# A hybrid attention block on one core: first loads in halves, a different rank for the written-out order, last scalings moved to ScalarE

## The chip, the cores and the metric

The kernel runs on one core of a Trainium2 chip. The core has five engines that run side by side and meet at semaphores: TensorE (PE; its weight loads are listed as PEld), VectorE (DVE), ScalarE (ACT), GpSimd (POOL) and SyncE (SP), which here only issues DMAs. ACT and POOL can issue DMAs as well, each on a queue of its own. The metric is the device time of one execution in microseconds (us), lower is better. Three runs of the kernel before took 426.47, 428.28 and 426.45 us; their median is 426.47.

## What is computed

One layer of an encoder on x of 512 tokens by 1024 channels, all in float32:

```python
h = rmsnorm(x, norm_g)
(q_lat, c_kv, k_rope, z_a, q_b, k_b, v_b, z_b,
 q_idx, k_idx, w_idx, gate_a, gate_b) = split(h @ w_in)
# branch a: 8 heads of latent attention, chunk-causal (chunks of 64)
q  = rmsnorm(q_lat) @ w_uq ; kv = rmsnorm(c_kv) @ w_ukv ; rotary part added
y_a = softmax(mask(q k)) v * silu(z_a)
# branch b: an indexer scores keys, each query keeps its 128 best ones
score = sum_h relu(q_idx_h k_idx) * w_idx_h ; keep the top 128
y_b = softmax(kept(q_b k_b) + rel_bias) v_b * silu(z_b)
merged = sigmoid(gate_a) * (y_a @ w_o_a) + sigmoid(gate_b) * (y_b @ w_o_b)
out = rmsnorm(x + merged @ w_out, final_g)
```

## The kernel before

**Precision.** A float32 product is made of three products of rounded operands. Each operand is split into a high part (rounded by a copy on ACT, `act`) and a low part (the rest, a subtraction on DVE or POOL, `lo_part`, or `stt` where a scale goes with it, as in `split_scaled`). `mm3` (line 405) issues high*high, high*low and low*high into one PSUM bank. So nearly every matmul waits for an ACT instruction and for a DVE instruction behind it.

**Who sets the order.** The order of each engine's instructions is written out while the kernel is built, by a planner (`Flow`, lines 134 to 242). The work is a set of generator functions, each spawned as a thread with a priority, which yield steps (`Step`: one or more engines that could do it, with a duration each), requests for buffers (`Get`) and conditions (`Until`). `Flow.run` (line 183) repeatedly takes the step with the smallest key: the planned start, which `Flow.start` works out from when the engine is free and when operands were written and read, plus a small term for the priority and a random nudge drawn from the seed `DRAW` (71). It emits that instruction and books its planned end. The engines then run their lists in order on the chip, whatever the true durations are. DMAs on SP have a planned queue too (`hw`, `dma`).

**The head.** `loads` (line 528) issues on SP, for each of the eight 128-row slices of transposed x, the slice (`xT`, 256 KB) and the weights of the first projections: `w_qi` for the indexer's queries (256 columns) and `w_kvl` for latents, indexer keys and weights (328 columns). The very first `w_qi` goes on ACT's queue (`setup`, line 484). `setup_pool` (line 502) issues `ident` (for transposes) and `g_lat` on POOL's queue; the planner places them after the fourth slice, but in POOL's own list only two memsets stand ahead of them. `warm_up` gives PE 15 products of zeros. `early_x` (line 618) scales each slice by norm_g and splits it; the first slice's high part is made in three column pieces (256 to 512, 128 to 256, 0 to 128: `PIECES`) and its low part as a whole. `early_w` (line 633) splits the weights through `split_w` (line 605). `early_mm` (line 646) runs the products slice by slice: for the first, high*high of the indexer's queries by pieces, then with the low parts, then the 328 columns for four token tiles with `mm3`; for each later slice six and twelve products.

**The middle.** `fetcher`, `splitter` and `multiplier` walk a list of weight jobs (`QUEUE`). Attention heads run in two lanes per branch beside them: scores, softmax, transposes on PE (`turn`, line 412), a split of the transposed probabilities (`s_ph`), products with the values. Selecting the best keys is a chain of DVE instructions (`topk`, lines 818 to 830). The eight tiles of branch a's gate, after their tanh on ACT (`gate`, line 1170), are stored to DRAM by SP (line 1184) and fetched back later.

**The tail.** `output` (line 1814) computes the last product by a scheme of seven block products. For each token tile, `finish` (line 1760) adds the product to x, has the square summed (`square` on ACT, or, for the last piece, a DVE reduction at line 1768), and multiplies by the final gain. `scale_out` (line 1786) adds the sums, takes the power -0.5 on POOL (`power`, line 374), scales the first half of the columns on DVE and the second on ACT, and stores each half from SP. The tiles end in the order 2, 3, 0, 1; tiles 1 and 3 have three pieces each, tiles 0 and 2 two.

Of the kernel before, what the change touches and what calls it, by code (L numbers as in the profile page):

```python
# [133 lines left out]
class Flow:  # L134
# [9 lines left out]
    def __init__(self):  # L144
        self.free = {"PE": 0.6, "ACT": 0.6, "DVE": 0.6, "POOL": 0.6, "SP": 0.6}
        self.hw, self.dma = 0.6, 0.0
        self.pbias = -1.0
        self.port = 0.0
        self.threads = []

        self.draw = random.Random(DRAW)

# [30 lines left out]
    def run(self, stop=None):  # L183
        while self.threads:
# [15 lines left out]
            for t in self.threads:  # L200
                if isinstance(t.req, Step):
                    for i, (eng, dur, emit) in enumerate(t.req.options):
                        s = self.start(t.req, eng)
                        key = (s + BIAS * t.prio + t.nudge, t.prio)
# [22 lines left out]
            else:  # L227
# [3 lines left out]
                if step.moves and eng == "ACT":  # L231

                    end += 1.8 + step.moves
# [14 lines left out]
DRAW = 71  # L248
# [4 lines left out]
def tile_block(ctx: ExitStack, tc: tile.TileContext, a: dict, out: bass.AP, bias_dram: bass.AP):  # L253
# [181 lines left out]
    def act_dma(dst, src):  # L435
        step = Step([("ACT", 0.06, lambda: nc.scalar.dma_start(dst.ap, src))], bufs(dst), [])
        step.moves = 4.0 * dst.n * dst.ap.shape[0] / 360000
        return step
# [89 lines left out]
    def loads():  # L528
        for kp in range(4):
            for kk in range(2):  # L530
                k = 2 * kp + kk
                x = yield slot("x")
                yield dma(x.all.f, a["xT"][k])
                xt[k] = x
                if k == 0:
                    yield dma(normg.all, a["norm_g"])
                if kp == 0:
                    cq, ck = slice(256 * kk, 256 * kk + 256), slice(328 * kk, 328 * kk + 328)
                    if k:
                        rq = yield slot("er")  # L540
                        yield dma(rq.all.f[:, :256], a["w_qi"][kp][:, cq])
                        eraw["q", k] = rq.all.f[:, :256], True
# [11 lines left out]
            if kp == XAT:  # L554
                spawn(x_squares(), PSQ)
                yield is_done("x loads")
# [48 lines left out]
    def split_w(raw, w, dst, key, cls="w", cap=None, release=False, early=False):  # L605
# [3 lines left out]
        yield act(hi[:, :w], raw)  # L609
# [6 lines left out]
    first_x = {}  # L616

    def early_x():
        for k in range(NK):
            yield Until(lambda: k in xt)  # L620
            hi = yield slot("xg")
            lo = yield slot("xg")
            if k == 0:

                for piece in PIECES:
                    yield act(hi[:, piece], xt[k].all.f[:, piece], AF.Copy, scale=normg[:, k : k + 1])
                    first_x[piece.start] = hi
                yield stt(lo.all, xt[k].all.f, normg[:, k : k + 1], hi.all.f, ALU.mult, ALU.subtract)
# [4 lines left out]
    def early_w():  # L633
        for k in range(NK):
# [3 lines left out]
            yield Until(lambda: ("kv", k) in eraw)  # L638
            raw, last = eraw["kv", k]
            yield from split_w(raw, 328, ewkv, k, "w", WCAP, last, True)  # L640
# [5 lines left out]
    def early_mm():  # L646
# [6 lines left out]
        for i, piece in enumerate(PIECES[:2]):  # L653
            yield Until(lambda: piece.start in first_x)
            for m in range(2):
                yield mm(qi_ps[m][:, piece], [(ewq[0][0][:, m * P : m * P + P], first_x[piece.start][:, piece])], not i, False)
        for k in range(NK):
            yield Until(lambda: k in xg and k in ewq)

            xk = cut(xg[k], SCORED)  # L660
            w = [cut(ewq[k], slice(m * P, m * P + P)) for m in range(2)]
            if k == 0:

                for cw, cx in ((1, 0), (0, 1)):
                    for m in range(2):
                        yield mm(qi_ps[m][:, SCORED], [(w[m][cw], xk[cx])], False, False)
            else:
                for m in range(2):
                    yield mm3(qi_ps[m][:, SCORED], w[m], xk, False, k == NK - 1)
# [4 lines left out]
            for t in range(NT):  # L674
                yield mm3(kv_ps[t][:, :328], cut(xg[k], TOK[t]), cut(ewkv[k], slice(0, 328)), k == 0, k == NK - 1)
# [494 lines left out]
    def gate(name, c, how=proj):  # L1170


        def take(ps):
# [7 lines left out]
            if c in away and name == "w_ga":  # L1181
                yield dma(spilt(c), s.all.f)
# [525 lines left out]
    def out_job(product, c):  # L1708
# [3 lines left out]
        def prep(job):  # L1712
# [47 lines left out]
    def finish(t, half, c0, c1, ps, nth, last, keep=False):  # L1760
# [6 lines left out]
        if last:  # L1767
            step = Step([("DVE", 0.1 + 0.00104 * r.n, lambda: nc.vector.tensor_tensor_reduce(
                junk.tile[:, : r.n], r.ap, r.ap, op0=ALU.mult, op1=ALU.add, scale=1.0, scalar=0.0,
                accum_out=ssf[t].tile[:, nth : nth + 1]))], [junk, ssf[t]], bufs(r))  # L1770
# [4 lines left out]
        else:  # L1775
            spawn(square(t, r, nth), 0)
# [3 lines left out]
        done.add(("g", t, nth))  # L1780

# [4 lines left out]
    def scale_out(t, count):  # L1786
# [3 lines left out]
        yield ts(rs[:, 0:1], ssf[t][:, 0:1], ssf[t][:, 1:2], D * EPS, ALU.add, ALU.add)  # L1790
        if count == 3:
            yield is_done(("sq", t, 2))
            yield tt(rs[:, 0:1], rs[:, 0:1], ssf[t][:, 2:3], ALU.add)
        done.add(("sum", t))
        yield power(rs[:, 0:1])
        yield Until(lambda: all(("g", t, i) in done for i in range(count)))
        for half, engs in ((0, ("DVE",)), (1, ("ACT",))):
            x = rg[t, half].all.f
            yield scale_by(x, x, rs[:, 0:1], engs)
            yield dma(out[TOK[t], half * 512 : (half + 1) * 512], x)  # L1800
# [157 lines left out]
NWARM = 15  # L1958
# [101 lines left out]
```

## Time and profile before

| what | value |
|---|---|
| median of three runs | 426.47 us |
| the profiled execution, whole | 427.16 us |
| its span, first to last instruction | 425.4 us |
| mean granted TensorE clock | 0.995 |
| PE, PEld, DVE, ACT, POOL busy | 98%, 86%, 89%, 62%, 26% |
| HBM read and written | 50.49 MB, 4.21 MB |

The profile is of one execution. An engine's busy time is the time in which at least one of its instructions ran. The ends of matmuls are modelled, and they overlap, so a busy PE isn't PE at its full rate; the distance between starts says more. In a timeline each row has a start, a length, engine, line, operation, what is written and read, and in brackets the engine's idle time before it with what ended it. A line is often that of a helper (L400 is every matmul, L302 and L311 every ACT copy or activation, L328 and L339 the DVE operations, L427 every DMA from SP), so the names of the tiles tell more: `s_xg` is the scaled x of the head, `s_w` a split weight, `s_x` a raw slice, `s_er` and `raw` raw weights, `s_p` probabilities, `sm` small columns, `s_rg` the finished rows.

### The profile page before, as it was taken

What the parts mean: (1) busy time and instruction counts of PE and PEld (TensorE: products, weight loads), DVE (VectorE), ACT (ScalarE), POOL (GpSimd) and SP (SyncE); (2) the same over time, 40 slices, a digit from 0 to 9 for tenths busy, and PEclk for the clock granted to TensorE, in tenths of its full rate; (3) what the DMA queues carried; (4) which work ended last, traced back from release to release, by engine and by line L of the source; (5) the groups of instructions that cost most, each with busy time, mean ns of one, the idle gap of its engine ahead of it and who ended that gap; (6) DMA issues with size and microseconds to landing.
All of it is one profiled execution on the core that took longest, in us unless ns stands there. A gap on an engine that the chain in (4) does not pass through costs nothing.

```text
span 425.4 us, 7106 instructions
## 1 busy us (share of the span) xinstructions
PE 415.3 (98%) x2313; PEld 363.9 (86%) x2313; DVE 380.5 (89%) x815; ACT 262.2 (62%) x587; POOL 109.5 (26%) x131
## 2 busy tenths in 40 slices
PE   8999999999999999999999999999999999999993
PEld 6999868889888888888899988998998888888883
DVE  4789899999999999999879888988799757999995
ACT  6778786585573758544864677494598524436624
POOL 1037865455355723121300101000010002210212
PEclk9999999999999999999999999999999999999998
DMA  8973137817255450285243525425523887453705
GB/s 258 394 278 112 52 100 207 230 45 186 82 139 148 127 160 1 79 256 173 63 128 121 171 79 157 146 65 178 146 79 124 266 322 252 143 180 106 242 0 197
DMA packets 30277, 65.89 MB, mean 155 GB/s; under 512 B 4648, under 2 KB 5688, under 8 KB 30240
## 3 DMA queue, kind: packets, MB, share of 16 engines
q1 hardware_dynamic: 29264, 64.08, 48.5%
q0 software_dynamic: 832, 1.22, 0.9%
q8 instruction: 18, 0.29, 0.3%
q14 instruction: 19, 0.16, 0.1%
q10 hardware_dynamic: 144, 0.13, 0.1%
HBM read 50.49 MB, written 4.21 MB: 129 GB/s over the span
## 4 chain that ended last, share of the span: by engine, by line
PE 54%; DVE 30%; DMA 7%; ACT 4%; issue 4%; POOL 0%; POOLq 0%; SPq 0%; DVEq 0%; ACTq 0%
PE ps L400 50%; DVE mask L826 4%; DMA raw<-w_out 4%; DVE sm L825 3%; PE ps L417 2%; DVE sm L1474 2%; DVE s_ph L328 2%; DVE s_mg L328 2%; DVE s_wsum L328 1%; DMA s_sig<-bias_scratch 1%; DVE s_tmp L328 1%; ACT s_p L311 1%; DVE s_pair L328 1%; DVE s_wo L328 1%; DVE s_w L328 1%
## 5 line engine op out<-in xcount | busy, mean ns | idle before, releaser
L400 PE MATMUL ps<-s_h,s_w 128*128 128x512 f32 (+1 forms) x732 | 170.9, 379 | 0.0
L400 PEld LDWEIGHTS ps<-s_h,s_w 128*128 128x128 f32 x732 | 127.8, 189 | 21.8 <-issue 0.3
L302 ACT CAST s_w<-raw 128x512 fp32r<-128x512 f32 (+3 forms) x124 | 71.6, 593 | 17.8 <-DVE raw L328 9.2
L330 POOL TENSOR_TENSOR s_w<-raw,s_w 128x512 fp32r<-128x512 f32 (+2 forms) x35 | 44.7, 1284 | 130.1 <-ACT s_w L302 123.9
L328 DVE TENSOR_TENSOR s_w<-raw,s_w 128x512 fp32r<-128x512 f32 (+2 forms) x89 | 58.7, 670 | 5.3 <-ACT s_w L302 4.7
L400 PE MATMUL ps<-s_ys,s_w 128*128 128x512 f32 x192 | 43.7, 389 | 0.0
L400 PEld LDWEIGHTS ps<-s_ys,s_w 128*128 128x128 f32 x192 | 36.0, 188 | 7.5
L311 ACT ACTIVATE s_p<-s_p,sm 128x384 f32<-128x384 f32 (+3 forms) x54 | 29.2, 559 | 6.8 <-DVE sm L1571 5.6
L400 PE MATMUL ps<-s_wo,s_mg 128*128 128x512 f32 (+1 forms) x156 | 33.0, 373 | 0.0
L400 PE MATMUL ps<-s_w,s_xg 128*128 128x328 f32 (+1 forms) x192 | 32.5, 323 | 0.0
L400 PEld LDWEIGHTS ps<-s_wo,s_mg 128*128 128x128 f32 x156 | 27.6, 188 | 5.2
L400 PEld LDWEIGHTS ps<-s_w,s_xg 128*128 128x128 f32 x192 | 31.4, 188 | 0.0
L328 DVE TENSOR_TENSOR s_ph<-ps,s_ph 128x384 fp32r<-128x384 f32 (+1 forms) x48 | 27.4, 590 | 2.5 <-ACT s_ph L302 2.3
L302 ACT CAST s_ph<-ps 128x384 fp32r<-128x384 f32 (+1 forms) x48 | 23.5, 514 | 5.5 <-PE ps L417 4.2
L311 ACT ACTIVATE s_p<-ps,sm 128x128 f32<-128x128 f32 (+3 forms) x32 | 16.8, 527 | 15.5 <-DVE sm L1474 15.1
L826 DVE MATCH_REPLACE8 mask<-sm,mask 128x384 f32<-128x384 f32 (+2 forms) x48 | 25.8, 540 | 0.0
L825 DVE MAX8 sm<-mask 128x8 f32<-128x384 f32 (+2 forms) x48 | 25.5, 547 | 0.1
L400 PE MATMUL ps<-s_ph,vv 128*128 128x512 f32 (+3 forms) x128 | 24.9, 325 | 0.0
L417 PE MATMUL ps<-ident,s_p 128*128 128x128 f32 x160 | 24.2, 275 | 0.5 <-DVE s_p L358 0.3
L417 PEld LDWEIGHTS ps<-ident,s_p 128*128 128x128 f32 x160 | 18.8, 140 | 4.7 <-ACT s_p L311 1.0
L400 PEld LDWEIGHTS ps<-s_ph,vv 128*128 128x128 f32 x128 | 20.6, 189 | 2.1 <-DVE s_ph L328 0.2
L400 PE MATMUL ps<-s_lat,s_w 128*128 128x512 f32 x78 | 20.5, 398 | 0.0
(197 smaller groups left out, 737.5 us busy)
## 6 DMA issues: line engine op xcount, KB each, us to landing
raw<-w_out SPq DMA_DIRECT2D x18, 512.0 KB, 4.0
s_op<-s_op SPq DMA_DIRECT2D x36, 128.0 KB, 2.3
raw<-w_ga SPq DMA_DIRECT2D x8, 512.0 KB, 4.5
raw<-w_gb SPq DMA_DIRECT2D x8, 512.0 KB, 4.4
raw<-w_o SPq DMA_DIRECT2D x16, 256.0 KB
s_x<-xT SPq DMA_DIRECT2D x8, 256.0 KB, 4.9
s_xn<-x SPq DMA_DIRECT2D x8, 256.0 KB, 5.7
bias_scratch<-s_sig SPq DMA_DIRECT2D x8, 256.0 KB, 2.5
```

Of the source, the lines that this page charges most:

```text
L302: nc.scalar.copy(dst.ap, src.ap)
L311: nc.scalar.activation(dst.ap, src.ap, func, **kw)
L328: opts.append(("DVE", 0.07 + 0.00104 * x.n, lambda: nc.vector.tensor_tensor(dst.ap, x.ap, y.ap, op=op)))
L330: opts.append(("POOL", 0.15 + 0.0021 * x.n, lambda: nc.gpsimd.tensor_tensor(dst.ap, x.ap, y.ap, op=op)))
L400: nc.tensor.matmul(ps.ap, l.ap, r.ap, start=start and i == 0, stop=stop and i == len(pairs) - 1, skip_group_check=more)
L417: nc.tensor.transpose(d.ap, s.ap, ident.tile)
L825: yield Step([("DVE", t, lambda: nc.vector.max(m8.tile, work.tile))], [m8], [work])
L826: yield Step([("DVE", t, lambda: nc.vector.match_replace(work.tile, m8.tile, work.tile, MARK))], [work], [m8])
L1474: yield Step([("DVE", 0.07 + 0.00104 * n, lambda: nc.vector.tensor_reduce(mx.tile[:, 1:2], ps.tile[:, :n], op=ALU.max, axis=AX.X, negate=T ...
```

## The change

- **First x.** Slice 0 is loaded as two column halves into one tile: columns 256 to 512 by SP, columns 0 to 256 by ACT, behind `w_qi`. `early_x` makes high and low part piece by piece. `early_mm` takes the products of slice 0 piece by piece, with high*high and low*high of the 328 columns ahead of high*low, tile 3 first. The cast of the first `w_kvl` waits in the plan for the pieces of x.
- **First w_qi.** Its high part is made on DVE with a multiplication by 1, not on ACT.
- **ident and g_lat** are issued by SP, behind all slices of x.
- **Order.** The key of a PE or SP step uses `settled`: the time at which its operands will have been left alone by other engines for 2 us (PE; 1 us after SP) or 1 us (SP). The planned start itself isn't changed. `DRAW` is 53, `NWARM` 14, and the planner books ACT's DMAs as a queue.
- **Gate stores** of branch a are issued by ACT.
- **Tail.** The squares on ACT get priority -50. For tile 1 the DVE reduction of its last piece starts from the sum of the other pieces, so the addition behind it goes. Tile 0's first half is scaled on ACT. Tile 1's second half is stored from ACT.
- In the weights of the last product, product 4's sums wait in the plan until product 6's are split.

```diff
+    def settled(self, step, eng, start):
+        s = start
+        for b in (*step.ins, *step.outs):
+            for e, t in ((b.by, b.w), *b.reads.items()):
+                if e != eng and e in SETTLE[eng]:
+                    s = max(s, t + self.lat(e, eng) + SETTLE[eng][e])
+        return s
...
-                        key = (s + BIAS * t.prio + t.nudge, t.prio)
+                        key = ((self.settled(t.req, eng, s) if eng in SETTLE and s < math.inf else s) + BIAS * t.prio + t.nudge, t.prio)
...
-DRAW = 71
+DRAW = 53
+PSQUARE = -50
+SETTLE = {'PE': {'DVE': 2.0, 'ACT': 2.0, 'POOL': 2.0, 'SP': 1.0}, 'SP': {'DVE': 1.0, 'ACT': 1.0, 'POOL': 1.0}}
...
+    def act_move(dst, src):
+        d = dst.ap if isinstance(dst, View) else dst
+        step = Step([("ACT", 0.3, lambda: nc.scalar.dma_start(d, src.ap))], bufs(dst), bufs(src))
...
         eraw["q", 0] = rq.all.f[:, :256], True
+        yield Until(lambda: x0)
+        x0.append(Buf(x0[0].tile, "x0"))
+        yield act_dma(x0[1].all.f[:, LO], a["xT"][0][:, LO])
+        xt[0] = x0[0]
...
-        yield Until(lambda: 3 in xt)
-        yield from pool_dma(ident.all, a["ident"])
-        yield from pool_dma(glat.all, a["g_lat"])
...
+                    yield dma(x.all.f[:, HI], a["xT"][0][:, HI])
+                    x0.append(x)
...
             if kp == XAT:
+                yield dma(ident.all, a["ident"])
+                yield dma(glat.all, a["g_lat"])
...
+        if dst is ewq and key == 0:
+            yield Step([("DVE", 0.1 + 0.00052 * w, lambda: nc.vector.tensor_scalar(
+                hi.tile[:, :w], raw.ap, 1.0, None, ALU.mult))], [hi], bufs(raw))
+        else:
+            yield act(hi[:, :w], raw)
...
+                    yield act(part[0][:, piece], x, AF.Copy, scale=normg[:, 0:1])
+                    first_x[i] = part
+                    yield stt(part[1][:, piece], x, normg[:, 0:1], part[0][:, piece].f, ALU.mult, ALU.subtract)
...
-            yield Until(lambda: ("kv", k) in eraw)
+            yield Until(lambda: ("kv", k) in eraw and len(first_x) == len(PIECES))
...
+                for t in (3, 2, 1, 0):
+                    i = (2, 1, 0, 0)[t]
+                    yield Until(lambda: i in first_low)
+                    x = cut(first_x[i], TOK[t])
+                    yield mm(kv_ps[t][:, wide], [(x[0], first_kv[0][:, wide]), (x[1], first_kv[0][:, wide])], True, False)
+                yield Until(lambda: k in ewkv)
+                for t in range(NT):
+                    yield mm(kv_ps[t][:, wide], [(first_x[(2, 1, 0, 0)[t]][0][:, TOK[t]], ewkv[k][1][:, wide])], False, False)
...
-                yield dma(spilt(c), s.all.f)
+                yield act_move(spilt(c), s.all.f)
...
-                    yield Until(lambda: 2 * c + i in sums)
+                    yield Until(lambda: 2 * c + i in sums and (product == 6 or (6, 2 * c + i) in right))
...
-                junk.tile[:, : r.n], r.ap, r.ap, op0=ALU.mult, op1=ALU.add, scale=1.0, scalar=0.0,
-                accum_out=ssf[t].tile[:, nth : nth + 1]))], [junk, ssf[t]], bufs(r))
+                junk.tile[:, : r.n], r.ap, r.ap, op0=ALU.mult, op1=ALU.add, scale=1.0, scalar=s.tile[:, 0:1],
+                accum_out=s.tile[:, 1:2]))], [junk, s], [r.buf, s])
...
-            spawn(square(t, r, nth), 0)
+            spawn(square(t, r, nth), PSQUARE)
...
-        for half, engs in ((0, ("DVE",)), (1, ("ACT",))):
+        for half, engs in ((0, ("ACT",) if t == 0 else ("DVE",)), (1, ("ACT",))):
...
+            if t == 1 and half:
+                yield Step([("ACT", 0.06, lambda: nc.scalar.dma_start(dst, x.ap))], [], bufs(x))
...
-NWARM = 15
+NWARM = 14
```

More of the change, by code (lines that the diff above doesn't have):

```diff
@@ L231, in run @@
                 if step.moves and eng == "ACT":
-                    end += 1.8 + step.moves
+                    self.adma = max(self.adma, end + (1.1 if end < 7.3 else 1.5)) + step.moves * (SLOW if end < 7.3 else 1.0)
+                    end = self.adma + 1.0
                 elif step.moves:
@@ L637, in early_w @@
             yield from split_w(raw, 256, ewq, k, "w", WCAP, last, True)
[L638 removed]
+            yield Until(lambda: ("kv", k) in eraw and len(first_x) == len(PIECES))
             raw, last = eraw["kv", k]
[L640 removed]
+            yield from split_w(raw, 328, ewkv, k, "w", WCAP, last, True, first_kv)
         for k in range(NK):
@@ L661, in early_mm @@
             w = [cut(ewq[k], slice(m * P, m * P + P)) for m in range(2)]
[L662 to L669, printed above, removed]
+            for m in range(2):
+                yield mm3(qi_ps[m][:, SCORED], w[m], xk, False, k == NK - 1)
             put(*ewq[k])
```

81 lines of the change are left out of this document (56 added, 25 removed).

## The prediction

> **What bounds the kernel now.** I read the page's busy line first.
>
> ```profile
> span 425.4 us, 7106 instructions
> PE 415.3 (98%) x2313; PEld 363.9 (86%) x2313; DVE 380.5 (89%) x815; ACT 262.2 (62%) x587; POOL 109.5 (26%) x131
> ```
>
> TensorE (PE) is idle for 425.4 - 415.3 = 10.1 us. All products stay in number and size, so the time can fall only by what PE loses: before its first useful product, in waits on the way, and after its last one. The timeline shows where the 10.1 us lie. First its head (start, length, engine, line, operation; in brackets the idle time before it and what ended it):
>
> ```profile
> 0.73 0.41 ACTq L436 DMA_DIRECT2D s_er<-w_qi  x1
> 0.73 0.40 SPq L427 DMA_DIRECT2D s_x<-xT  x1
> 1.05 3.38 PE L498 MATMUL ps<-zeros 128*128 128x256 bf16 x15 [1.05 <-DVE neghalf L454]
> 1.32 0.76 POOL L431 DMA_DIRECT2D ident<-ident  x1 [0.19 <-issue]
> 2.12 0.43 SPq L427 DMA_DIRECT2D s_x<-xT  x1
> 4.04 0.40 ACT L302 CAST s_w<-s_er 128x256 fp32r<-128x256 f32 x1 [1.38 <-DMA s_er<-w_qi]
> 4.36 1.09 ACT L311 ACTIVATE s_xg<-s_x,normg 128x256 fp32r<-128x256 f32 x3
> 4.91 1.16 PE L400 MATMUL ps<-s_xg,s_w 128*128 128x256 f32 x6 [0.48 <-ACT s_xg L311]
> 5.43 0.47 ACT L302 CAST s_w<-s_er 128x328 fp32r<-128x328 f32 x1
> 5.48 0.75 DVE L339 SCALAR_TENSOR_TENSOR s_xg<-s_x,normg,s_xg 128x512 fp32r<-128x512 f32 x1 [0.57 <-ACT s_xg L311]
> 6.28 0.62 PE L400 MATMUL ps<-s_xg,s_w 128*128 128x384 f32 x2 [0.21 <-DVE s_xg L339]
> 6.74 1.95 PE L400 MATMUL ps<-s_w,s_xg 128*128 128x328 f32 x12
> 7.05 0.72 ACT L311 ACTIVATE s_xg<-s_x,normg 128x512 fp32r<-128x512 f32 x1 [1.15 <-DMA s_x<-xT]
> 7.81 0.75 DVE L339 SCALAR_TENSOR_TENSOR s_xg<-s_x,normg,s_xg 128x512 fp32r<-128x512 f32 x1 [1.17 <-ACT s_xg L311]
> 8.52 1.40 PE L400 MATMUL ps<-s_xg,s_w 128*128 128x384 f32 x6
> ```
>
> The reader is to see two chains. One ends at PE's 6.28: w_qi lands at 4.04, ScalarE (ACT) rounds it (0.40), then rounds x in three pieces until 5.45, VectorE (DVE) makes the low part of x whole (5.48 to 6.23). The other ends at PE's 8.52, where the second slice of x begins: it lands at 7.05, ACT takes it to 7.77, DVE to 8.56. PE has products until 8.69, so both chains end at about the same moment there, and neither can be shortened alone.
>
> The middle has three waits of any size. I put with each the row ahead of it, and one stretch of plain 512-wide products for their pace:
>
> ```profile
> 360.00:370.00 10.00, 10.00 (x46) 8.29 (x45) 9.79 (x18) 4.56 (x9) 1.12 (x1) 1.00 0.39 133
> ...
> 56.35 0.65 PE L803 MATMUL ps<-s_qs,s_qs 96*128 96x512 f32 x2
> 57.97 0.31 PE L852 MATMUL ps<-s_oh,rbs 64*8 64x320 f32 x1 [0.97 <-DVE mask L339]
> ...
> 55.16 2.11 DVE L328 TENSOR_TENSOR s_tmp<-s_tmp,s_tmp 32x512 f32<-32x512 f32 x1
> ...
> 166.07 0.94 PE L400 MATMUL ps<-s_h,s_w 128*128 128x512 f32 x3
> 167.26 0.81 PE L417 MATMUL ps<-ident,s_p 128*128 128x128 f32 x4 [0.26 <-DVE s_p L358]
> ...
> 212.73 0.44 PE L417 MATMUL ps<-ident,s_p 128*128 128x128 f32 x2 [0.25 <-ACT s_p L311]
> ```
>
> 46 products in 10 us is 0.22 us each. Two of them from 56.35 make the next one due at 56.79; it began at 57.97, 1.18 late. Three from 166.07 make 166.73 due; 167.26 is 0.53 late. The third wait I take at its shown 0.25. Together 1.96 us. The ends of matmuls are modelled, so the bracketed 0.97 + 0.26 + 0.25 = 1.48 says a little less; the starts are the better measure. (The first one stands behind a DVE addition of 32x512 that took 2.11 us.)
>
> The tail, from PE's last products:
>
> ```profile
> 417.82 0.75 PE L400 MATMUL ps<-s_wo,qhi 128*128 128x256 f32 x5
> 419.03 0.41 DVE L339 SCALAR_TENSOR_TENSOR s_xr<-ps,s_xr 128x256 f32<-128x256 f32 x1
> 419.16 0.72 ACT L311 ACTIVATE s_rg<-s_rg,sm 128x512 f32<-128x512 f32 x1 [0.30 <-POOL sm L378]
> 419.36 0.48 DVE L358 TENSOR_SCALAR s_rg<-s_rg,sm 128x512 f32<-128x512 f32 x1
> 419.75 0.42 DVE L1768 CUSTOM_DVE_ANT_0 junk<-s_xr 128x256 f32<-128x256 f32 x1
> 420.21 0.16 DVE L328 TENSOR_TENSOR sm<-sm,ssf 128x1 f32<-128x1 f32 x1
> 420.45 0.66 POOL L378 TENSOR_TENSOR sm<-sm,neghalf 128x1 f32<-128x1 f32 x1 [1.32 <-DVE sm L328]
> 421.15 0.72 ACT L311 ACTIVATE s_rg<-s_rg,sm 128x512 f32<-128x512 f32 x1 [1.27 <-POOL sm L378]
> ...
> 416.35 6.12 SPq L427 DMA_DIRECT2D out<-s_rg  x8
> ```
>
> PE ends at 418.57; 6.8 us follow it. 1.05 (start) + 0.48 + 0.21 (head) + 1.48 (middle) + 6.8 (tail) make the 10.1.
>
> **The change, part by part.** Durations are those of the profiled execution, which took 427.16 us (1.76 more than its span). The three runs have a median of 426.47, 0.69 less; I work out differences and take them from the median.
>
> **Head.** The first x comes in column halves, one from ACT's queue behind w_qi, one from SP's; ident and glat leave the POOL queue, where nothing held them back, and go on SP's behind the last slice of x. What they do there is seen in the windows of the head (after the busy times: granted clock, share of the DMA engines, GB/s) and the size of ident:
>
> ```profile
> 3.50:4.00 0.50, 0.50 (x4) 0.33 (x3) 0.00 (x0) 0.00 (x0) 0.00 (x0) 1.00 1.01 250
> 4.00:4.50 0.50, 0.43 (x3) 0.00 (x0) 0.02 (x1) 0.46 (x2) 0.00 (x0) 1.00 1.02 126
> 4.50:5.00 0.50, 0.09 (x1) 0.09 (x1) 0.41 (x1) 0.50 (x2) 0.00 (x0) 1.00 0.65 180
> ...
> 6.00:6.50 0.50, 0.29 (x2) 0.22 (x2) 0.50 (x2) 0.00 (x0) 0.00 (x0) 1.00 1.02 367
> ...
> ident<-ident POOLq DMA_DIRECT2D x1, 64.0 KB, 4.1
> ```
>
> From 3.5 to 5.0 the engines moved (250 + 126 + 180) x 0.5 = 278 KB; at the 367 GB/s of 6.0 they would have moved 550. The lack is 272 KB, or 0.74 us at 367. ident was issued at 1.32 and took 4.1 us to land, so it lies over this stretch. If only its bytes go, the second slice lands 64 / 367 = 0.17 us sooner; if the whole slump goes, 0.74. The Trainium skill, "DMA: Bandwidth & Descriptors", section Latency and other measured facts, says that some DMA engines are usually slower, guesses at the rings of GpSimd's software-made descriptors as the cause, and calls it specific to that path. The trace agrees in kind (126 GB/s at a share of 1.02); by that page the sum would be the 0.74.
>
> What PE could use of it: w_qi rounded by DVE takes ACT's 0.40 away. The nearest row for DVE:
>
> ```profile
> L358 DVE TENSOR_SCALAR s_p<-s_p,sm 128x256 f32<-128x256 f32 x5 | 1.7, 348 | 0.1
> ```
>
> So w is ready at 4.04 + 0.35 = 4.39, and ACT begins x when x and norm_g are there: after 4.04 and no later than 4.36; I take 4.2. PE begins at about 4.75 instead of 4.91. The low parts now come by pieces behind DVE's rounding (0.35) and w's low part (0.43), which end at 4.82; pieces of 256, 128 and 128 columns (0.41 for 256 in the tail's 419.03 row; 0.3 for 128 is an estimate) end near 5.25, 5.55 and 5.85. The products with the low part of x (columns from 128 on) start near 5.6, not 6.28, and the twelve 328-wide ones near 5.95, not 6.74. kv's cast is put behind the pieces of x: on ACT it began at 5.43 just behind them already, so nothing is added, and its 0.47 ends at 5.9, in time. PE would then be through at 5.95 + 1.95 = 7.9, 0.8 before its 8.69. The second slice must follow: 0.17 to 0.74 earlier. Beside it the six products from 8.52 took 1.40, where six 384-wide ones at 0.22 x 384 / 512 need 1.0; half of that may come back, 0.2 more. Later slices are not short: one is 256 KB of x, 128 of w_qi and 164 of w_kvl, 1.5 us at 367 GB/s, and PE needs 1.0 + 1.95 for it. **Head: 0.75 us**, with 0.17 and 1.1 as ends; the value stands near the upper bound of the landing, since the slump is what the row shows.
>
> ident and glat pass SP's loads of x by rows; these are delayed by two issues (0.43 each) and 64 KB, which were moved before as well, only sooner. Who waits: the squares, and behind them the latents. PE has the slices' products meanwhile (eight times 2.95 us). Nothing counted. One warm-up matmul less: nothing, the granted clock is 1.00 in all these rows.
>
> **Order.** The planner now ranks a PE step by when its operands have been done for 2 us (a SP step for 1 us), and draws other tie-breaks. This moves most instructions a little. What it can win is the 1.96 us of waits, and some small ones that the brackets hide; I put the end at 2.5. What it can lose is bounded by another wait like the largest: -1.2. All three rows are waits for an operand made just before, which is what the rank steers away from; I take 70% of 1.96, **1.4 us**.
>
> **ACT's stores of the gates.** Eight leave SP's queue for ACT's:
>
> ```profile
> L427 SPq DMA_DIRECT2D bias_scratch<-s_sig x8: 320/337/584, 55.3 to 196.7; - x8
> ```
>
> ACT pays 0.41 each (row of 0.73), 3.3 us over 140 us, and first waits for its own tanh. Behind it queue casts of weights and of probabilities, for which DVE and then PE wait. ACT is busy 62%, and the slack hides it: 0. If the cover were gone, 3.3 us and the waits. SP is freed of a wait per gate; nothing on PE waits for a DMA, so 0 there too. The squares' priority and product 4's wait for product 6 change order alone: 0.
>
> **Tail.** Tile 0's first half goes from DVE to ACT, so 0.48 leaves DVE ahead of the reduction: it can begin at about 419.5, not 419.75 (0.25). The sum starts from the partial sum, so the addition goes and the power follows the reduction's read-out: 420.45 becomes 420.25 (0.2). ACT gets a second 0.72 from 419.88 to 420.60; the last power ends at 420.45 - 0.45 + 0.66 = 420.66, so it is just free. The last store is issued by ACT itself instead of second on SP: between 0.1 and 0.35; 0.1 taken. **Tail: 0.55 us.** Ends: 0.2 (the second scaling slips behind the power) and 0.8.
>
> Sum: 0.75 + 1.4 + 0.55 = 2.7. 427.16 - 2.7 = 424.5 for a run like the profiled one; from the median, **423.8 us**, 0.6% faster. About 0.5% (2.1 us, 424.3) is what a measurement of this kernel can tell from no change.
>
> **Rivals.**
>
> 1. The order wins nothing: the new one has as many waits elsewhere. For it: each wait comes from one late operand (a 2.11 us addition), which a rank with fixed lags doesn't foresee. Against: 0.53 and 0.25 are waits of transposes on fresh probabilities. Only 0.75 + 0.55 = 1.3 is left: 425.2.
>
> 2. The halves and the moved loads don't do what they say: the second slice lands no earlier, since the same bytes go through the same engines. For it: share 1.02 at 4.0, the engines were not free. Against: at 4.5 the share is 0.65. Then PE finishes the first slice early and waits to 8.5: head 0, 1.95 left: 424.5. The Trainium skill, "DMA: Bandwidth & Descriptors", section Issuing engines are not separate DMA queues, says that DMAs of all issuers interleave on the same 16 engines and that several issuers save only issue time. No run here shows a load split so; by that rule the halves give nothing, and only ident's way matters.
>
> 3. Slower: ACT's queue becomes what PE waits for. Each store holds ACT for its tanh's write and 0.41 of issue, some 0.6 us, 4.9 for eight. It decides once ACT has no idle time between a gate and the next cast that PE needs. Against it: 38% idle. For it: the third wait is already on ACT. 426.47 - 2.7 + 4.9 = 428.7.
>
> **How the numbers follow.** Forecast 0.62, rival 1 0.17, rival 2 0.14, rival 3 0.07. The forecast's own ends: 1.1 + 2.5 + 0.8 = 4.4 gives 422.1; the likely lower side of each (0.4, 0.8, 0.3) gives 425.0. Rival 1 with a small head (0.17) and its tail is 425.7, with one new wait of 0.6 426.3. The range is 422.1 to 426.3 and leaves out rival 3 and little else. Of the forecast 0.51 lies below 424.3 and 0.11 above, of rival 2 0.06 and 0.08; rival 1 is within 0.5%. Faster 0.57, same 0.36, slower 0.07.
>
> **What would show it.** Head: the second slice's rounding on ACT starts near 6.3 instead of 7.05, and PE's first 384-wide run of that slice near 7.8 instead of 8.52; 250 to 180 GB/s between 3.5 and 5.0 should be 300 or more. Order: the bracketed idle times of PE between 10 and 410 add up to about 0.4 instead of 1.48. Tail: from PE's last end to the span's end 6.3 instead of 6.8. ACT: busy time up by nothing, waits of PE on ACT not above 0.5. I am wrong if PE waits in new places, if the slump stays without the POOL loads, or if the last scaling finds ACT occupied.

## The result, and the profile after

The changed kernel took 424.86 us (median of 15 runs, 424.19 to 427.08). The kernel before, run beside it, took 428.22 us (15 runs, 426.27 to 429.81). The ratio is 0.9935, with a 95% interval of 0.9917 to 0.9953: 0.65% faster, where 0.6% had been forecast. The forecast of 423.8 us stood on the median of three runs (426.47); the 15 runs put the kernel before 1.75 us higher, so the changed kernel lies 1.06 us above the forecast, within its range, while the medians differ by 3.36 us where 2.7 had been forecast. The profiled execution took 424.27 us, its span 422.5 us. The page's first lines:

```profile
span 422.5 us, 7070 instructions
PE 414.6 (98%) x2312; PEld 364.4 (86%) x2312; DVE 372.9 (88%) x797; ACT 265.3 (63%) x596; POOL 124.3 (29%) x139
```

The span fell by 2.89 us. It is cut in three at two events of PE's timeline, the first 384-wide product of the second slice and the last product's end:

| part | before | after | gain | forecast |
|---|---|---|---|---|
| start to PE's second slice (head) | 8.52 | 8.07 | 0.45 | 0.75 |
| second slice to PE's last end (middle) | 410.04 | 408.17 | 1.87 | 1.4 |
| PE's last end to the span's end (tail) | 6.83 | 6.26 | 0.57 | 0.55 |

The sum, 2.89, is near the forecast's 2.7; the shares are not. First the head, in the timeline:

```profile
3.63 0.29 DVE L637 TENSOR_SCALAR s_w<-s_er 128x256 fp32r<-128x256 f32 x1 [2.62 <-DMA s_er<-w_qi]
3.92 1.09 ACT L323 ACTIVATE s_xg<-s_x,normg 128x256 fp32r<-128x256 f32 x3 [0.76 <-DMA normg<-norm_g]
4.46 0.48 DVE L351 SCALAR_TENSOR_TENSOR s_xg<-s_x,normg,s_xg 128x256 fp32r<-128x256 f32 x1 [0.53 <-ACT s_xg L323]
4.48 1.96 PE L412 MATMUL ps<-s_xg,s_w 128*128 128x256 f32 x8 [0.26 <-ACT s_xg L323]
4.86 0.42 DVE L340 TENSOR_TENSOR s_w<-s_er,s_w 128x256 fp32r<-128x256 f32 x1
...
6.00 0.72 ACT L323 ACTIVATE s_xg<-s_x,normg 128x512 fp32r<-128x512 f32 x1 [0.22 <-DMA s_x<-xT]
6.27 1.97 PE L412 MATMUL ps<-s_w,s_xg 128*128 128x328 f32 x12
8.07 1.23 PE L412 MATMUL ps<-s_xg,s_w 128*128 128x384 f32 x6
```

DVE rounds w_qi, so ACT is free for x as soon as norm_g lands (3.92). PE begins at 4.48, 0.43 earlier, and the second slice is there at 6.00, 1.05 earlier. But from PE's first useful product to the second slice it still takes 3.59 us (3.61 before). PE runs into the second slice without a bracket, so the landing doesn't set that start. It didn't before either: the row of 8.52 has no bracket. The loads in the windows (columns as in the prediction):

```profile
3.50:4.00 0.50, 0.50 (x4) 0.17 (x2) 0.29 (x1) 0.08 (x1) 0.00 (x0) 1.00 0.72 180
4.00:4.50 0.50, 0.24 (x3) 0.03 (x1) 0.04 (x1) 0.50 (x2) 0.00 (x0) 1.00 0.74 117
4.50:5.00 0.50, 0.50 (x2) 0.50 (x3) 0.50 (x2) 0.50 (x2) 0.00 (x0) 1.00 0.67 237
```

The 300 GB/s of the forecast were not there. The share fell to 0.7, so the engines had less to move; but 117 GB/s at a share of 0.74 is still less than half of what the same share would move at the rate of 6.0 (367 at 1.02). So the slump stayed without the POOL loads, which the prediction had named as a sign of being wrong. PE's waits between 10 and 412 us are down to one row (total, times, longest):

```profile
PE ps L1547 <- DMA s_op<-kpel: 0.4, 1, 0.4
```

Before, the same list held 1.0, 0.3 and 0.2, the three waits of the prediction. The tail:

```profile
416.07 2.70 ACT L323 ACTIVATE s_rg<-s_rg,sm 128x512 f32<-128x512 f32 x4
416.33 0.41 DVE L351 SCALAR_TENSOR_TENSOR s_xr<-ps,s_xr 128x256 f32<-128x256 f32 x1
416.78 0.49 DVE L1825 CUSTOM_DVE_ANT_0 junk<-s_xr,sm 128x256 f32<-128x256 f32 x1
417.35 0.67 POOL L390 TENSOR_TENSOR sm<-sm,neghalf 128x1 f32<-128x1 f32 x1 [0.93 <-DVE sm L1825]
418.05 0.49 DVE L370 TENSOR_SCALAR s_rg<-s_rg,sm 128x512 f32<-128x512 f32 x1 [0.44 <-POOL sm L390]
418.80 0.34 ACTq L1869 DMA_DIRECT2D out<-s_rg  x1
```

The power follows the reduction's read-out with no addition between, and ACT's four scalings stand close together: ACT is just free for the last, as forecast. The last store is issued 2.56 us after PE's end, not 3.52. That is 0.96 won, of which 0.57 is left at the span's end.

### The profile page after: what moved, and what is told of

Same layout as the page of the kernel before. It is cut to its first block, busy times and chain, and to the rows that moved or that the text cites. A ratio compares the mean times of both kernels' runs of the same rounds, so it can differ in the third digit from the quotient of the medians.

```text
span 422.5 us, 7070 instructions
## 1 busy us (share of the span) xinstructions
PE 414.6 (98%) x2312; PEld 364.4 (86%) x2312; DVE 372.9 (88%) x797; ACT 265.3 (63%) x596; POOL 124.3 (29%) x139
## 3 DMA queue, kind: packets, MB, share of 16 engines
q0 software_dynamic: 768, 1.15, 0.9%
## 4 chain that ended last, share of the span: by engine, by line
PE 77%; DVE 7%; DMA 6%; ACT 4%; issue 2%; SPq 2%; POOL 0%; POOLq 0%; DVEq 0%; ACTq 0%
PE ps L412 69%; PE ps L429 4%; DMA s_x<-xT 3%; SPq L439 2%; DVE s_tmp L351 2%; DVE s_tmp L340 2%; DMA s_xn<-x 1%; PE ps L1547 1%; PE ps L1548 1%; PE ps L1546 1%; ACT ps L323 1%; DMA raw<-w_ql 1%; DMA s_op<-kpel 1%; ACT junk L323 1%; DVE s_h L340 1%
## 5 line engine op out<-in xcount | busy, mean ns | idle before, releaser
L342 POOL TENSOR_TENSOR s_w<-raw,s_w 128x512 fp32r<-128x512 f32 (+2 forms) x39 | 48.5, 1253 | 47.6 <-ACT s_w L314 43.7
L340 DVE TENSOR_TENSOR s_w<-raw,s_w 128x512 fp32r<-128x512 f32 (+2 forms) x85 | 55.9, 670 | 4.4 <-ACT s_w L314 3.9
L323 ACT ACTIVATE s_p<-s_p,sm 128x128 f32<-128x128 f32 (+3 forms) x62 | 32.8, 552 | 4.9 <-DVE sm L1626 4.3
L342 POOL TENSOR_TENSOR s_p<-s_bias,mask 128x128 f32<-128x128 f32 (+2 forms) x5 | 4.4, 890 | 75.5 <-DMA s_bias<-bias_scratch 75.5
L429 PE MATMUL ps<-ident,s_p 128*128 128x128 f32 x160 | 23.1, 273 | 0.0
L1529 DVE TENSOR_REDUCE sm<-ps 128x1 f32<-128x128 f32 (+3 forms) x32 | 14.8, 480 | 8.2 <-PE ps L1548 7.8
```

Of the source, the lines that this page charges most:

```text
L323: nc.scalar.activation(dst.ap, src.ap, func, **kw)
L340: opts.append(("DVE", 0.07 + 0.00104 * x.n, lambda: nc.vector.tensor_tensor(dst.ap, x.ap, y.ap, op=op)))
L342: opts.append(("POOL", 0.15 + 0.0021 * x.n, lambda: nc.gpsimd.tensor_tensor(dst.ap, x.ap, y.ap, op=op)))
L429: nc.tensor.transpose(d.ap, s.ap, ident.tile)
L1529: yield Step([("DVE", 0.07 + 0.00104 * n, lambda: nc.vector.tensor_reduce(mx.tile[:, 1:2], ps.tile[:, :n], op=ALU.max, axis=AX.X, negate=T ...
```

## The experiments

PE's start of the second slice, its time from there to its last end, and the tail are read from each run's one profiled execution. "Planned end" is the planner's own booked end of PE in us, worked out while the kernel is built: 408.6 for the kernel before, 407.7 for the changed one. The runs were made in four groups, each with the kernel before beside them (its medians: 428.22, 427.09, 427.9 and 427.94), so between groups the ratios compare better than the times.

**The rank alone (e3).** The kernel before with `settled` and `SETTLE`, seed 71 kept.

```diff
-                        key = (s + BIAS * t.prio + t.nudge, t.prio)
+                        key = ((self.settled(t.req, eng, s) if eng in SETTLE and s < math.inf else s) + BIAS * t.prio + t.nudge, t.prio)
```

> The kernel before with the settled rank of PE and SP steps alone, the same seed. Theory (the rank is what removes PE's waits): PE's idle time between 10 and 410 us falls from 1.48 to below 0.6 us, PE's last end comes 1.5 to 2 us sooner than 418.6, ratio about 0.996. Rival (the waits went by the luck of the new seed): idle time stays above 1.0 us, ratio 0.998 to 1.003.

It took 437.81 us, ratio 1.023 (1.0189 to 1.027). PE's waits:

```profile
PE ps L410 <- DVE s_wo L338: 4.1, 1, 4.1
PE ps L410 <- DVE s_w L338: 2.7, 5, 1.4
```

The rank steered PE into longer waits than it removed. The longest cost more than itself. It ended at 418.72; behind it, in windows of 3.4 us (granted clock, DMA share and GB/s stand last):

```profile
419.70:423.10 3.40, 3.40 (x9) 2.67 (x9) 0.00 (x0) 0.00 (x0) 0.00 (x0) 0.50 0.00 0
423.10:426.50 3.40, 3.40 (x16) 2.72 (x16) 2.66 (x6) 1.45 (x4) 0.47 (x1) 1.00 0.00 0
```

At a granted clock of 0.50, PE got through 9 products where 16 fit, about 1.5 us more. The planner had seen part of the loss: planned end 412.0.

**The seed without the rank (e4).** The changed kernel with `SETTLE` empty.

```diff
-SETTLE = {'PE': {'DVE': 2.0, 'ACT': 2.0, 'POOL': 2.0, 'SP': 1.0}, 'SP': {'DVE': 1.0, 'ACT': 1.0, 'POOL': 1.0}}
+SETTLE = {}
```

> The changed kernel without the settled rank, its seed and all else kept. Theory (the rank): PE's idle time between 10 and 410 us rises from 0.37 to 1 us or more, and 1.5 us of the gain go: ratio to before about 0.9975. Rival (the seed and the head's shift made the order good): idle time stays near 0.4 us, ratio near 0.9935 as with the whole change.

440.06 us, ratio 1.0286 (1.0255 to 1.0316), with every other edit in place:

```profile
PE ps L412 <- DVE s_wo L340: 5.1, 1, 5.1
PE ps L858 <- DVE s_lat L351: 2.6, 1, 2.6
PE ps L429 <- ACT s_p L323: 1.7, 1, 1.7
```

Here too the granted clock was 0.50 for 3.4 us behind the wait of 2.6 (from 56.2) and for 6.8 us during and behind the wait of 5.1 (from 411.2). Neither half gained anything alone. Each edit reshuffles the order, and these two seeds fit one set of edits each. Both orders were planned late (412.0, and 413.7 here), and on the chip they lost two to three times what the plan showed. So the rank had to be judged between plans of about equal length.

**The rank at an equal plan (e7).** The kernel before with the rank and seed 13 (planned 408.7).

```diff
-DRAW = 71
+DRAW = 13
```

> The kernel before with the settled rank alone, and a seed (13) with which the planner's own end of PE is 408.7, as good as that of the kernel before (408.6); the rank with the old seed had 412.0 and measured 2.3% slower. Theory (the rank brings the run nearer to the plan): PE's idle time between 10 and 410 us falls below 0.8 us and PE's last end, corrected for the first slices, comes 1 us or more sooner than in the kernel before; ratio 0.996 to 0.998. Rival (the plan's end alone decides): ratio 1.000, idle 1.5 us.

428.94 us, ratio 1.0037 (1.0007 to 1.0067), single runs from 426.55 to 432.73. In the profiled execution, its fastest, PE's bracketed idle time between 10 and 410 us fell to 0.16, as the theory had it, but one wait had only moved, to 410.3, and the time didn't fall:

```profile
PE ps L410 <- ACT s_wo L312: 1.1, 1, 1.1
```

**No rank, with good plans (e8, then e10).** The changed kernel with `SETTLE` empty and seed 0 (planned 408.1), then seed 2 (408.28).

```diff
-DRAW = 53
+DRAW = 0
```

> The changed kernel without the rank, with a seed (0) for which the planner's end of PE is 408.1, near the changed kernel's 407.7; without the rank and with its own seed it had 413.7 and measured 2.9% slower. Theory (the rank): PE's idle time between 10 and 410 us is 1.5 us or more and the time 1.0 to 2.0 us above the changed kernel; ratio to before 0.996 to 0.999. Rival (any order with as good a plan does it): ratio 0.9935 to 0.995.

428.89 us, ratio 1.0031 (1.0012 to 1.0049), middle 411.49, bracketed idle 1.85: the way of the theory, with a loss larger than it had.

> The changed kernel without the preference for settled operands, seed 2, planned end 408.28 us: a second sample beside the first such kernel, whose middle took 411.49 us. Theory (the preference is worth time beyond what the plan shows): middle of 410.5 us or more, idle of 1.5 us or more on products that wait for VectorE or ScalarE, total 426.5 to 428.5 us. Rival (only the plan's quality counts): middle 408.3 to 409.2 us, total near 425 us.

429.49 us, ratio 1.0041 (1.0009 to 1.0074). Its profiled execution was its fastest (426.91), with a middle of 409.74, where the theory wanted 410.5 or more and the rival 409.2 or less: neither. The total went beyond both. Its waits are on fresh probabilities and sums, the kind the rank steers away from:

```profile
PE ps L429 <- DVE s_tmp L340: 0.7, 1, 0.7
PE ps L429 <- ACT s_p L323: 0.7, 1, 0.7
```

**The rank with another seed (e9).** The changed kernel with seed 5, planned end 407.72, the same as with 53.

```diff
-DRAW = 53
+DRAW = 5
```

> The changed kernel with another seed of the planner (5 instead of 53), whose order is a different one but plans the same end of TensorE (407.72 us). Theory (a settled-operand order with a good plan is what gave the middle its 1.4 us): from the second slice to TensorE's last end about 408.3 us, idle after 10 us below 0.8 us, total 424.3 to 425.5 us. Rival (the seed was a lucky pick among orders that the plan cannot tell apart): 409.5 us or more in the middle, idle of 1.5 us or more, total 426 to 428 us.

426.12 us, ratio 0.9959 (0.9931 to 0.9987): faster than before, and 1.3 us behind seed 53. The time lies above the theory's range and at the lower end of the rival's. The profiled execution has the rival's marks too (middle 411.56, bracketed idle 3.2), but it was the slowest (429.27) and isn't typical; it shows where such an order can break:

```profile
PE ps L412 <- ACT s_rbc L314: 2.0, 1, 2.0
```

With the changed kernel's other edits, the two orders with the rank took 424.86 and 426.12, the two without 428.89 and 429.49. The plans differ by 0.4 to 0.6 us, the times by 2.8 to 4.6, and the intervals of the ratios don't touch. In the kernel before, the rank gave nothing at an equal plan. So the rank goes with the gain here, but two orders a side don't make it a rule. The seed may be worth as much as the 1.3 us between the two equal plans; their ratios differ by 0.0024 with overlapping intervals. How seed 53 was chosen isn't on record; if it was the best of several that were measured, part of its lead is selection.

**ident and g_lat alone (e2)** moved to SP behind the slices; order otherwise that of before.

```diff
-        yield Until(lambda: 3 in xt)
-        yield from pool_dma(ident.all, a["ident"])
-        yield from pool_dma(glat.all, a["g_lat"])
...
+                yield dma(ident.all, a["ident"])
+                yield dma(glat.all, a["g_lat"])
```

> The kernel before with ident and g_lat moved from POOL's queue to SP's, behind the slices of x; nothing else changes its place. Theory (the POOL loads slow the other loads, and PE is bound by two chains at once): the rate from 4.0 to 4.5 us is 250 GB/s or more instead of 126, the second slice's rounding on ACT starts near 6.3 instead of 7.05, but PE's second slice starts at 8.4 to 8.5 and not before, since its first slice still ends late; time within 0.2 us of before. Rival (only the bytes count): the rounding starts near 6.9. Second rival (the landing was the bound): PE's second slice starts near 7.8 and the time falls by 0.6 us.

427.34 us, ratio 0.9995 (0.9973 to 1.0017). The timeline:

```profile
5.74 0.72 ACT L311 ACTIVATE s_xg<-s_x,normg 128x512 fp32r<-128x512 f32 x1
...
6.53 1.96 PE L400 MATMUL ps<-s_w,s_xg 128*128 128x328 f32 x12
8.33 1.23 PE L400 MATMUL ps<-s_xg,s_w 128*128 128x384 f32 x6
```

The second slice is there by 5.74 without any halves, as early as with them, and PE comes to it at 8.33 all the same, out of an unbroken run of products. Landing sooner didn't help: PE wasn't waiting for it. From 4.0 to 4.5 us the loads moved 246 GB/s, near the theory's 250; but two runs that kept ident on POOL moved 226 (the tail alone) and 237 (the rank alone) there, so that isn't shown to be the move's doing.

**The tail alone (e1)**, on the kernel before, all else in the same order.

```diff
-        for half, engs in ((0, ("DVE",)), (1, ("ACT",))):
+        for half, engs in ((0, ("ACT",) if t == 0 else ("DVE",)), (1, ("ACT",))):
...
+            if t == 1 and half:
+                yield Step([("ACT", 0.06, lambda: nc.scalar.dma_start(dst, x.ap))], [], bufs(x))
```

> The kernel before with the edits of the tail alone; every other instruction keeps its place on its engine. Theory (the tail is worth what stands between PE's last end and the span's end, 6.83 us before and 6.26 after the whole change): 6.2 to 6.4 us there, the time 0.55 us below the kernel before, ratio about 0.9987. Rival (the last store and not the scaling chain sets the end, so shortening the chain gives nothing): 6.8 us there and ratio 1.000.

426.8 us, ratio 0.9992 (0.9971 to 1.0014): nothing that can be told from zero. The profiled execution was longer than that of before (428.27), and not in the tail (6.67 instead of 6.83): PE reached the second slice only at 10.17. In PE's timeline and in windows of 2 us:

```profile
4.82 2.50 PE L401 MATMUL ps<-s_xg,s_w 128*128 128x256 f32 x8 [0.38 <-ACT s_xg L312]
7.12 3.22 PE L401 MATMUL ps<-s_w,s_xg 128*128 128x328 f32 x12
10.17 1.03 PE L401 MATMUL ps<-s_xg,s_w 128*128 128x384 f32 x5
```

```profile
6.00:8.00 2.00, 2.00 (x8) 1.99 (x8) 1.63 (x5) 1.39 (x3) 0.00 (x0) 1.00 1.05 318
10.00:12.00 2.00, 2.00 (x15) 2.00 (x14) 1.50 (x3) 2.00 (x5) 0.00 (x0) 1.00 1.03 401
```

The head's instructions are those of the kernel before, yet its twelve 328-wide products take 3.22 us instead of 1.95. From 6 to 8 us eight products touch the window, from 10 to 12 fifteen, and the column of the granted clock says 1.00 for both. Between starts, 328-wide products lie 273 ns apart until about 9.85 us and 150 ns after it. So the array ran at about half rate and changed late, and the clock's column doesn't show it; the spacing does. The column reads 1.00 where the trace has no record of the clock: this run's record begins at 9.89 us. In the profiled execution of before it begins at 5.11 us, in that of the changed kernel at 5.63, where the spacings change too. The three runs below ask what moves it.

**Two more warm-up products in the changed kernel (e5)** (16), all else in the same order.

```diff
-NWARM = 14
+NWARM = 16
```

> The changed kernel with 16 warm-up products instead of 14; all else keeps its place. Theory (the array's clock opens late in some executions, at 5 to 5.5 us or only near 10 us, because PE pauses between the warm-up and its first product: in the tail-only run twelve 328-wide products took 273 ns each and the second slice began at 10.17 instead of 8.5): without the pause the clock opens early in each execution; of the times none lies 1.5 us above the lowest, where 4 of 15 of the changed kernel did, and the median falls by 0.2 to 0.5 us. Rival (the pause does not matter, the phase of the gate does): the same share of times lies high, and the median rises by 0.2 us for the two products more.

424.79 us, ratio 0.9939 (0.9919 to 0.9958), six runs from 424.12 to 425.25. Full rate began near 4.5 us, PE's second slice at 7.63. No run lay 1.5 us above the lowest, as the theory had it (five of the changed kernel's 15 did; the text on record counts four), but six runs are few, and the median, which was to fall, is the changed kernel's.

**Two more in the kernel before (e6)** (17).

```diff
-NWARM = 15
+NWARM = 17
```

> The kernel before with 17 warm-up products instead of 15, which reach to its first product; all else keeps its place. Theory (late opening after a pause): its times, of which about half lie near 428.4 and half near 426.5, all come near 426.5; median 0.5 to 1.5 us below the kernel before. Rival (the phase of the gate): times stay in two groups, median unchanged.

427.28 us, ratio 0.9991 (0.9973 to 1.0008). Full rate began near 5.9 us although PE had hardly paused, and 5 of 12 runs were still above 428. The pause isn't all of it.

**Four fewer in the changed kernel (e12)** (10).

```diff
-NWARM = 14
+NWARM = 10
```

> The changed kernel with 10 warm-up products instead of 15, all else in the same order, so that TensorE rests for about 1.1 us longer ahead of its first useful product. Theory (full rate comes only after a stretch of unbroken work): the 256-wide products go on at 213 ns until 7.5 to 10 us, and the total is 0.5 to 2 us above the changed kernel's. Rival (the opening has nothing to do with the warm-up): full rate from about 5.7 us as in the changed kernel, total within 0.3 us of it.

(The text on record counts from 15; it is 14, and PE's pause is 0.88 us longer.) 426.01 us, ratio 0.9951 (0.9925 to 0.9977), against 0.9935 (0.9917 to 0.9953). With the order unchanged, 1.15 us of the gain are gone by the medians and 0.7 by the ratios, whose intervals overlap. In the timeline:

```profile
4.51 2.50 PE L412 MATMUL ps<-s_xg,s_w 128*128 128x256 f32 x8 [1.14 <-ACT s_xg L323]
6.81 2.72 PE L412 MATMUL ps<-s_w,s_xg 128*128 128x328 f32 x12
9.36 1.21 PE L412 MATMUL ps<-s_xg,s_w 128*128 128x384 f32 x6
```

PE begins at the same moment (4.51 against 4.48) and has its operands, but comes to the second slice 1.29 us later: its 328-wide products lie 273 ns apart until 8.45 us. So it went in this execution as the theory said; over all runs the loss isn't clear of the noise.

**The gate stores back on SP (e11)**, at the same places, all else in the same order.

```diff
-        step = Step([("ACT", 0.3, lambda: nc.scalar.dma_start(d, src.ap))], bufs(dst), bufs(src))
+        step = Step([("ACT", 0.3, lambda: nc.sync.dma_start(d, src.ap))], bufs(dst), bufs(src))
```

> The changed kernel with the eight gate stores issued by SP at the same place, as before the change; all else in the same order. Theory (the stores on ScalarE cost nothing, as forecast): ScalarE busy 2.6 to 3 us less, total the same within 0.3 us, and TensorE's 0.4 us wait for the recalled slice at 84.2 us may stay. Rival (ScalarE's queue pays): 0.4 us or more faster.

424.28 us, ratio 0.9917 (0.9888 to 0.9946): the lowest median of the study, with an interval that overlaps the changed kernel's. The profiled executions differ by 0.14 us, 0.12 of it in the head; the middle is the same, 408.13 against 408.17, and one short wait replaces another:

```profile
PE ps L858 <- DMA s_qs<-s_th: 0.6, 1, 0.6
```

and the page's busy line:

```profile
PE 414.1 (98%) x2312; PEld 364.3 (86%) x2312; DVE 372.6 (88%) x797; ACT 264.5 (63%) x596; POOL 125.1 (30%) x139
```

The expected 2.6 to 3 us less of ACT's busy time didn't come (264.5 against 265.3): issuing a DMA isn't counted as busy. In the total, the stores on ACT cost between nothing and some 0.6 us; these runs can't say which.

## Why the prediction was right, and where not

The gain came out near the forecast, and the sum of the profiled pair (0.45 + 1.87 + 0.57 = 2.89) is near its 2.7. That the sum fits so well is partly luck: the head gave less than its term and the middle more.

- **Head: mis-sized, 0.75 forecast, 0.45 found.** Two steps were right: DVE's rounding freed ACT, and PE began at 4.48 (4.75 forecast). Over all heads of each kind the first product lies at 4.77 (five runs with the old head, 4.70 to 4.91) and 4.36 (eight with the new one, 4.17 to 4.51). The step that failed is "PE would be through at 5.95 + 1.95 = 7.9", with the second slice's landing as the thing to win. PE took as long from its first product as before. In the profiled run of before the products ran at full rate from near 5.1 us and stood still for operands; in that of the changed kernel the waits were gone, but the array ran at half rate until near 5.6: 256-wide products 214 ns apart, and the first 384-wide one 351 where later ones are 175. And w's low part on DVE (4.86) went behind the first low piece of x (4.46), not ahead of it as I had it.
- **The slump of the loads changes from execution to execution.** The forecast read 126 GB/s at 4.0 and a landing at 7.05 as properties of the kernel. The same loads landed (read from the start of the rounding) at 6.15, 5.87, 6.37 and 6.54 in the four other runs that kept them (e1, e3, e6, e7); the new loads at 5.34 to 6.25, mean 5.92 against 6.40. So the slice lands sooner by 0.5, within the forecast's ends, and ident's way alone brought as much in its one profile (5.74). The slump came without the POOL loads as well: from 4.0 to 4.5 us the five profiles with them moved 126 to 237 GB/s, the eight of the new loads 70 to 314. What makes it is open; the share of 1.02 is a mean over the 16 engines and can't show, as the prediction read it, that some of them were slow. The Trainium skill, "DMA: Bandwidth & Descriptors", section Issuing engines are not separate DMA queues, has DMAs of all issuers share the same engines; one execution agrees, in which loads that were not split landed as early. Rival 2 fell all the same: the slice did land sooner, and PE doesn't wait at its start.
- **"One warm-up matmul less: nothing, the granted clock is 1.00 in all these rows"** was a wrong reading. The column says 1.00 while products run at half rate, and with four warm-ups fewer the median was 1.15 us higher (0.7 by the ratios, with overlapping intervals). What one is worth was not measured.
- **Order: the size was right, the reason only in part.** Four runs in the old order (before, e1, e2, e6) have a middle of 410.04, 409.65, 409.36 and 409.67, mean 409.68; four in the changed order (after, e5, e11, e12) 408.17, 408.47, 408.13 and 408.43, mean 408.30. That is 1.4 us, and PE's bracketed idle time from 10 to 410 us went from 1.48 to 0.36 in the profiled pair (0.4 forecast), from 1.36 to 0.52 in the mean of these four and four. Whether the rank or the seed did it is not settled. But "the rank steers away from" such waits wasn't enough: with seed 71 kept it cost 2.3%, and the seed without the rank 2.9%. The bound given for a loss (1.2 us) was far too small; the largest single wait found was 5.1. Rival 1, waits elsewhere, is what the rank did in the kernel before.
- **Tail: 0.57 for 0.55, but the edits' own part isn't shown.** Tails differ by tenths with the same code. In the old order they were 6.83, 6.42 and 6.45 without the edits (before, e2, e6), mean 6.56, and 6.67 with them (e1): no gain. In the changed order, with the edits, they were 6.26, 6.25, 6.25 and 6.64 (after, e5, e11, e12), mean 6.35, 0.21 less; in other orders with the same edits 6.06 (e8), 6.38 (e4), 7.27 (e10) and 7.63 (e9). What stands in the order's last microseconds weighs more than the shorter chain, and the profiled run of before had the longest tail of its kind.
- **ACT's queue (rival 3): it did not become the bound.** PE's waits between 10 and 412 us name no ACT. ACT's busy time rose by 3.1, where "nothing" was forecast; since issuing isn't counted, that is other work that the new order gave to ACT, the tail's fifth scaling of 0.7 among it. A store holds ACT for 0.4 us, not rival 3's 0.6: one tanh of the changed kernel ends at 80.16 and ACT's next instruction begins at 80.56, with the issue between. The 0.2 for the tanh's write is shown by no run.

The medians differ by 3.36 us, the means above by 0.41 (first product) + 1.38 (middle) + 0.21 (tail), 2.0. What is left may lie in how often an execution starts late at full rate. Each kernel's runs fall into two groups some 2 us apart: of the kernel before 6 of 15 lie below 427.2 (mean 426.7), of the changed one 10 of 15 below 425 (mean 424.6), and these two lower groups differ by 2.1. The distance of the groups is about what e1 and e3 lost at the second slice (10.17 and 10.21, against 8.5 to 8.7 in the other old heads). The clock records fit: stretches at one granted clock last 3.41 us or a multiple (3.41 and 6.83 at 0.50 in the runs of the rank alone and the seed alone; 413.01 or 416.43, which is 121 or 122 times that, at 1.00 in most), so a head that misses one opening would run 3.41 us longer at half rate and lose 1.7. Only e1 and e3, and e12 with its shorter warm-up, show such an execution, so that link is argued, not shown; why the two kernels differ in the share stays open.

## What to carry to other kernels

Where an order is written out from a plan, test a new rule for it with the seed searched anew on both sides and with several seeds; one seed carried over can lose 2 or 3% and says nothing about the rule. A wait of PE that is long enough (2.6 us and more here, while 2.0 did nothing of the kind) costs more than itself, since half rate came with it. Before a stall in a head is put into a forecast, look whether a second execution has it, and read TensorE's rate from the distance between starts. An earlier load that nobody waits for gives nothing. Warm-up work up to the first real product may: with four products fewer the median was about 1 us higher, but two more, which closed the pause, gave nothing that can be told from zero in either kernel.

## What the runs showed of the hardware that I had not expected

- **The array's start at full rate moves from run to run.** 256-wide warm-up products lie 213 ns apart throughout. The records at full rate begin at 4.5 (e5), 5.0 (e4), 5.1 (before), 5.3 (e11), 5.5 (e2), 5.6 (after), 5.7 (e7), 5.8 (e10), 5.9 (e6), 6.5 (e9), 6.7 (e8), 8.5 (e12), 9.9 (e1) and 10.1 us (e3), and the spacings agree. Four of them (before, e1, e3, e7) have the old loads and 15 warm-up products. The Trainium skill, "TensorE: Matmul & The Clock Gate", section What's actually happening, states 1.2 GHz at first and 2.4 GHz once a free-running window of about 3.4 us has been busy. The trace agrees with the rates (256 / 1.2 GHz = 213 ns) and with an opening that differs from run to run; its spread of half a microsecond is smaller than the 5.0 us found here among these four.
- **PE fell back to half rate behind single waits.** Behind a wait of 2.56 us (e4) and one of 4.13 (e3) the granted clock was 0.50 for 3.4 us; it fell during the one of 5.13 (e4) and stayed there for 6.8. The wait of 2.0 in e9 left it at 1.00.
- **The last of two stores took longer to land when it came from a second queue.** Before, the last two stores were issued 0.42 us apart, and the last landed 2.26 us after its issue. From two queues they are 0.23 to 0.24 apart, and it took 2.77 in the changed kernel (2.46 to 2.78 in the eight others that store so and were measured). Each moves 256 KB, 0.7 us at 367 GB/s, so the second may well meet the first; of the 0.96 us won at the issue in the profiled pair, 0.51 went there.
